# Mean-square minus squared mean over 16384 rows: the first load cut in two by partitions, the first store issued from GpSimd's queue

## The chip, the cores and the metric

The kernel runs on one core of a Trainium2 chip. The metric is the device time of one execution in microseconds (us). Three runs of the kernel before are shown, and one further execution was recorded by the hardware profiler.

## What is computed

The input holds 32 x 512 rows of 1024 float32 numbers, 64 MiB in all. For each row the kernel returns the mean of the squares minus the square of the mean, which is the row's variance.

```python
batch, seq, dim = 32, 512, 1024
x = np.random.randn(batch, seq, dim).astype(np.float32)

def reference(x):
    mean_sq = np.mean(x**2, axis=-1)
    sq_mean = np.mean(x, axis=-1)**2
    return (mean_sq - sq_mean).astype(np.float32)
```

## The kernel before

The 16384 rows are laid over 128 partitions, 128 rows to a partition. What the code calls a column is one row in each of the 128 partitions: 128 x 1024 float32, 512 KiB. There are 128 columns, in two blocks (`BLOCKS`): the first 16 columns take rows 0 to 2047, so that partition p holds rows 16p to 16p+15, and the other 112 columns take the remaining rows in the same way. Each block is stored by one DMA at the end of the program text.

**Loads.** All loads go through SyncE's queue, in program order (`load`, L45). The body has 13 groups of eight columns (`NGROUPS`, `GROUP`): one DMA of 4 MiB each, 32 KiB to a partition, into a pool `xpool` of three buffers. So the first three loads are issued at once, and the load of group g+3 waits until the computation on group g has freed its buffer. The last 24 columns are loaded into a tile of their own (`xt_end`) by six DMAs of 6, 6, 4, 3, 2 and 1 columns (`END_LOADS`), and four half columns of 256 KiB. In this text b0 to b5 are those six, and h0 to h3 the four halves.

The framework gives each DMA of SyncE's and ScalarE's queues one of eight completion semaphores in rotation. Where a semaphore is used again, the issue of the later DMA waits for the landing of the earlier one.

**Computation.** A column is done by one of two engines. ScalarE (`act_cols`, L121 and L129) makes two passes over it: a Copy that accumulates the negative mean, and a Square with that as bias that accumulates the variance. VectorE (`dve_half`, L111) makes two `bn_stats` of 512 elements for it. In the body ScalarE takes three columns of an even group and two of an odd one, VectorE the other five or six. Every instruction works on all 128 partitions.

**Joining.** The partial statistics of VectorE are joined to a variance by ten small GpSimd instructions (`join`, L90 to L102), which is called three times: for the odd groups, for the even groups, and for the first two loads of the end. The last VectorE columns are finished by `bn_aggr` on VectorE (L169, L179).

**Stores.** `store` (L52) writes 128 x 16 results of block 0 from ScalarE's queue and 128 x 112 results of block 1 from SyncE's queue. The framework places an instruction by its engine's program order and by priorities: in the built program the store of block 0 stands on ScalarE between its work on group 12 and its work on b0, where it waits for the second join on GpSimd.

```python
    store(nc.scalar, BLOCKS[0])
    store(nc.sync, BLOCKS[1])
```

Of the kernel before, what the change touches and what calls it, by code (L numbers as in the profile page):

```python
# [11 lines left out]
def kernel(  # L12
# [8 lines left out]
    nc = tc.nc  # L21
    P = nc.NUM_PARTITIONS
# [4 lines left out]
    xf = x.flatten_outer_dims()  # L27
    N, D = xf.shape
# [6 lines left out]
    BLOCKS = [(0, SMALL, 0), (SMALL, ncols - SMALL, SMALL * P)]  # L35

    def block_of(c):
        return next(b for b in BLOCKS if b[0] <= c < b[0] + b[1])

    def load(dst, c0, n, f0=0, f=D):  # L40

        b0, pitch, row0 = block_of(c0)
        assert c0 + n <= b0 + pitch
        ap = [[pitch * D, P], [D, n], [1, f]] if n > 1 else [[pitch * D, P], [1, f]]
        nc.sync.dma_start(  # L45
            out=dst,
            in_=dataclasses.replace(xf, offset=(row0 + c0 - b0) * D + f0, ap=ap),
        )

    def store(engine, block):  # L50
        b0, pitch, row0 = block
        engine.dma_start(  # L52
            out=dataclasses.replace(out, offset=row0, ap=[[pitch, P], [1, pitch]]),
            in_=mv[:, 1, b0 : b0 + pitch],
        )

    GROUP = 8
    NGROUPS = 13
    END0 = GROUP * NGROUPS
    ACT_OF_GROUP = (3, 2)  # L60

    END_LOADS = [6, 6, 4, 3, 2, 1]
    END_WHO = "AADDDDAADDDDDADDDADADA"
# [12 lines left out]
    def stats_block(name, groups, each):  # L76

        st = opool.tile([P, groups * each, 2, 6], FP32, name=name)
        return st

    def join(st, groups, each, first, step, skip):

        n = groups * each
        part = st.rearrange("p n h (e s) -> p n (h e) s", s=3)
        mean, m2 = part[:, :, :, 1], part[:, :, :, 2]
        two = opool.tile([P, n, 2], FP32, name=f"two{first}")
        mu = opool.tile([P, n, 1], FP32, name=f"mu{first}")
        dev = opool.tile([P, n, 4], FP32, name=f"dev{first}")
        g = nc.gpsimd
        g.tensor_tensor(out=two, in0=mean[:, :, 0:2], in1=mean[:, :, 2:4], op=ALU.add)  # L90
        g.tensor_tensor(out=mu, in0=two[:, :, 0:1], in1=two[:, :, 1:2], op=ALU.add)
        g.tensor_scalar(out=mu, in0=mu, scalar1=0.25, scalar2=None, op0=ALU.mult)  # L92
        g.tensor_tensor(out=dev, in0=mean, in1=mu.to_broadcast([P, n, 4]), op=ALU.subtract)  # L93
        g.tensor_tensor(out=dev, in0=dev, in1=dev, op=ALU.mult)  # L94
        g.tensor_scalar(out=dev, in0=dev, scalar1=D / 4.0, scalar2=None, op0=ALU.mult)  # L95
        g.tensor_tensor(out=dev, in0=dev, in1=m2, op=ALU.add)  # L96
        g.tensor_tensor(out=two, in0=dev[:, :, 0:2], in1=dev[:, :, 2:4], op=ALU.add)  # L97
        g.tensor_tensor(out=mu, in0=two[:, :, 0:1], in1=two[:, :, 1:2], op=ALU.add)
        var = mv[:, 1, first : first + groups * step].rearrange(
            "p (g k) -> p g k", k=step  # L100
        )[:, :, skip : skip + each]
        g.tensor_scalar(  # L102
            out=var,
            in0=mu.rearrange("p (g k) o -> p g (k o)", k=each),
            scalar1=1.0 / D,
            scalar2=None,
            op0=ALU.mult,
        )
# [4 lines left out]
    def dve_halves(stats, xcol):  # L113
        dve_half(stats, 0, xcol[:, :H])
        dve_half(stats, 1, xcol[:, H:])

    def act_cols(cols):

        s = D ** -0.5
        for i, (xcol, c) in enumerate(cols):  # L120
            nc.scalar.activation(  # L121
                out=junk[i],
                in_=xcol,
                func=ACTF.Copy,
                scale=-s / D,
                accum_out=neg_mean[:, c : c + 1],
            )
        for i, (xcol, c) in enumerate(cols):
            nc.scalar.activation(  # L129
                out=junk[3],  # L130
                in_=xcol,
                func=ACTF.Square,
                scale=s,
                bias=neg_mean[:, c : c + 1],
                accum_out=mv[:, 1, c : c + 1],
            )

    body = []
    for par in range(2):
        groups = len(range(par, NGROUPS, 2))  # L140
        each = GROUP - ACT_OF_GROUP[par]
        body.append((stats_block(f"stats{par}", groups, each), groups, each))
    for g in range(NGROUPS):
        c0 = g * GROUP
        xt = xpool.tile([P, GROUP, D], FP32, name="xt")
        load(xt, c0, GROUP)
        skip = ACT_OF_GROUP[g % 2]
        act_cols([(xt[:, k, :], c0 + k) for k in range(skip)])
        st, _, each = body[g % 2]
        for k in range(skip, GROUP):  # L150
            dve_halves(st[:, g // 2 * each + k - skip, :, :], xt[:, k, :])
    for par, (st, groups, each) in enumerate(body):
        join(st, groups, each, par * GROUP, 2 * GROUP, ACT_OF_GROUP[par])

# [4 lines left out]
    for b, n in enumerate(END_LOADS):  # L159
        load(xt_end[:, k : k + n, :] if n > 1 else xt_end[:, k, :], END0 + k, n)  # L160
        mine = range(k, k + n)
        act_cols([(xt_end[:, j, :], END0 + j) for j in mine if END_WHO[j] == "A"])
        for j in mine:
            if END_WHO[j] == "D" and b < nb:
                dve_halves(st_end[:, b * each + j - k - skip, :, :], xt_end[:, j, :])
            elif END_WHO[j] == "D":
                stats = spool.tile([P, 2, 6], FP32, name="stats")
                dve_halves(stats, xt_end[:, j, :])
                nc.vector.bn_aggr(out=mv[:, :, END0 + j], in_=stats)  # L169
        if b == nb - 1:  # L170
            join(st_end, nb, each, END0, step, skip)
        k += n
    for j in range(k, ncols - END0):
        stats = spool.tile([P, 2, 6], FP32, name="stats")
        for h in range(2):
            xh = xt_end[:, j, h * H : (h + 1) * H]
            load(xh, END0 + j, 1, h * H, H)
            dve_half(stats, h, xh)
        nc.vector.bn_aggr(out=mv[:, :, END0 + j], in_=stats)  # L179

    store(nc.scalar, BLOCKS[0])
    store(nc.sync, BLOCKS[1])


# [28 lines left out]
```

## Time and profile before

| what | value |
| --- | --- |
| runs, median (lowest to highest) | 165.49 us (165.44 to 165.92) |
| profiled execution, first to last instruction (span) | 163.5 us |
| median run minus profiled span | 2.0 us |
| VectorE (DVE) busy | 106.1 us, 65% |
| ScalarE (ACT) busy | 94.9 us, 58% |
| GpSimd (POOL) busy | 10.2 us, 6% |
| read from HBM | 67.11 MB, 411 GB/s over the span |
| share of SyncE's load queue of 16 DMA engines' time | 96.3% |

The profiled execution has no time of its own apart from its span; what lies around the span is taken as the 2.0 us by which the median run exceeds it. TensorE is not used. In the profile's lines DVE is VectorE, ACT ScalarE, POOL GpSimd and SP SyncE; SPq and ACTq are the instructions with which SyncE and ScalarE issue DMAs. `x10` behind a line means ten instructions, and what stands behind `<-` in brackets is what ended the engine's idle time.

### The profile page before, as it was taken

The numbers are of one execution on the slowest core, as the hardware profiler recorded it, in microseconds if no ns is written. First come the engines' busy times: TensorE is split into PE (matmuls) and PEld (weight loads), VectorE is DVE, ScalarE is ACT, GpSimd is POOL, SyncE is SP. The second block draws the span as 40 slices with busy tenths as digits, with TensorE's granted clock in tenths as the row PEclk, the third lists the DMA queues.
The fourth block names the chain that finished last, engine by engine and source line by source line (L and its number), as shares of the span: only waits on it lengthen the run. The fifth ranks groups of instructions, "written<-read, shape, count | busy, mean of one in ns | idle before, by whom it ended". The sixth has DMA issues, their size and how long they took to land.

```text
span 163.5 us, 462 instructions
## 1 busy us (share of the span) xinstructions
DVE 106.1 (65%) x182; ACT 94.9 (58%) x165; POOL 10.2 (6%) x34
## 2 busy tenths in 40 slices
DVE  0008559393793917949097682949559396859993
ACT  3008756195733937349390693809755195499892
POOL 0000000000000000000000000000000635302200
DMA  7899898998999999999999999999999999999970
GB/s 257 385 481 417 385 513 385 417 481 385 481 417 385 485 409 393 497 393 425 465 393 473 417 393 505 393 401 489 393 465 425 421 391 475 391 440 409 408 291 14
DMA packets 3602, 67.19 MB, mean 411 GB/s; under 512 B 656, under 2 KB 656, under 8 KB 1296
## 3 DMA queue, kind: packets, MB, share of 16 engines
q1 hardware_dynamic: 3456, 67.17, 96.3%
q10 hardware_dynamic: 144, 0.01, 0.1%
q14 instruction: 2, 0.02, 0.0%
HBM read 67.11 MB, written 0.07 MB: 411 GB/s over the span
## 4 chain that ended last, share of the span: by engine, by line
DMA 79%; DVE 11%; ACT 8%; issue 0%; SPq 0%
DMA xt<-in_x_dram 62%; DMA xt_end<-in_x_dram 17%; DVE stats L111 10%; ACT junk L129 4%; ACT junk L121 4%; DVE mv L179 0%; SPq L45 0%
## 5 line engine op out<-in xcount | busy, mean ns | idle before, releaser
L111 DVE BATCH_NORM_STATS2 stats<-xt 128x6 f32<-128x512 f32 x142 | 85.5, 678 | 50.7 <-DMA xt<-in_x_dram 50.7
L121 ACT ACTIVATE junk<-xt 128x1024 bf16<-128x1024 f32 x33 | 34.5, 1046 | 59.2 <-DMA xt<-in_x_dram 59.2
L129 ACT ACTIVATE junk<-xt,neg_mean 128x1024 bf16<-128x1024 f32 x33 | 37.7, 1142 | 0.6
L111 DVE BATCH_NORM_STATS2 stats_end<-xt_end 128x6 f32<-128x512 f32 x16 | 9.7, 680 | 3.7 <-DMA xt_end<-in_x_dram 3.7
L121 ACT ACTIVATE junk<-xt_end 128x1024 bf16<-128x1024 f32 x8 | 8.4, 1046 | 5.0 <-POOL mv L102 4.2
L111 DVE BATCH_NORM_STATS2 stats<-xt_end 128x6 f32<-128x512 f32 x16 | 10.1, 666 | 0.1
L129 ACT ACTIVATE junk<-xt_end,neg_mean 128x1024 bf16<-128x1024 f32 x8 | 9.2, 1144 | 0.2
L90 POOL TENSOR_TENSOR two<-stats 128x72 f32<-128x72 f32 (+1 forms) x2 | 0.8, 406 | 131.3 <-DVE stats L111 131.3
L129 ACT ACTIVATION_READ_ACCUMULATOR junk<-xt,neg_mean 128x1 f32 x33 | 6.2, 186 | 0.0
L121 ACT ACTIVATION_READ_ACCUMULATOR junk<-xt 128x1 f32 x33 | 6.2, 186 | 0.0
L121 ACT ACT_TABLE_LOAD x1 | 1.3, 1283 | 0.7 <-PEq L197 0.7
L121 ACT ACTIVATION_READ_ACCUMULATOR junk<-xt_end 128x1 f32 x8 | 1.5, 186 | 0.0
L129 ACT ACTIVATION_READ_ACCUMULATOR junk<-xt_end,neg_mean 128x1 f32 x8 | 1.5, 186 | 0.0
L95 POOL TENSOR_SCALAR dev<-dev 128x144 f32<-128x144 f32 (+2 forms) x3 | 1.4, 472 | 0.3
L169 DVE BATCH_NORM_AGGREGATE mv<-stats 128x2 f32<-128x12 f32 x6 | 1.2, 203 | 0.1
L94 POOL TENSOR_TENSOR dev<-dev 128x144 f32<-128x144 f32 (+2 forms) x3 | 1.1, 362 | 0.2
L96 POOL TENSOR_TENSOR dev<-dev,stats 128x144 f32<-128x144 f32 (+1 forms) x2 | 1.1, 528 | 0.2
L93 POOL TENSOR_TENSOR dev<-stats,mu 128x144 f32<-128x144 f32 (+1 forms) x2 | 0.9, 470 | 0.2
L102 POOL TENSOR_SCALAR mv<-mu 128x36 f32<-128x36 f32 (+2 forms) x3 | 0.9, 287 | 0.3
L92 POOL TENSOR_SCALAR mu<-mu 128x36 f32<-128x36 f32 (+2 forms) x3 | 0.9, 284 | 0.3
L97 POOL TENSOR_TENSOR two<-dev 128x72 f32<-128x72 f32 (+2 forms) x3 | 0.8, 276 | 0.2
L90 POOL TENSOR_TENSOR two<-stats_end 128x16 f32<-128x16 f32 x1 | 0.2, 233 | 8.9 <-DVE stats_end L111 8.9
(9 smaller groups left out, 2.7 us busy)
## 6 DMA issues: line engine op xcount, KB each, us to landing
xt<-in_x_dram SPq DMA_DIRECT2D x13, 4096.0 KB, 22.2
xt_end<-in_x_dram SPq DMA_DIRECT2D x2, 3072.0 KB, 32.2
xt_end<-in_x_dram SPq DMA_DIRECT2D x1, 2048.0 KB, 40.0
xt_end<-in_x_dram SPq DMA_DIRECT2D x1, 1536.0 KB, 43.2
xt_end<-in_x_dram SPq DMA_DIRECT2D x1, 1024.0 KB, 45.1
xt_end<-in_x_dram SPq DMA_DIRECT2D x4, 256.0 KB, 15.3
xt_end<-in_x_dram SPq DMA_DIRECT2D x1, 512.0 KB, 36.7
out_dram<-mv SPq DMA_DIRECT2D x1, 56.0 KB, 1.6
```

The lines of the kernel that those rows point to most:

```text
L90: g.tensor_tensor(out=two, in0=mean[:, :, 0:2], in1=mean[:, :, 2:4], op=ALU.add)
L92: g.tensor_scalar(out=mu, in0=mu, scalar1=0.25, scalar2=None, op0=ALU.mult)
L93: g.tensor_tensor(out=dev, in0=mean, in1=mu.to_broadcast([P, n, 4]), op=ALU.subtract)
L94: g.tensor_tensor(out=dev, in0=dev, in1=dev, op=ALU.mult)
L95: g.tensor_scalar(out=dev, in0=dev, scalar1=D / 4.0, scalar2=None, op0=ALU.mult)
L96: g.tensor_tensor(out=dev, in0=dev, in1=m2, op=ALU.add)
L97: g.tensor_tensor(out=two, in0=dev[:, :, 0:2], in1=dev[:, :, 2:4], op=ALU.add)
L102: g.tensor_scalar(out=var, in0=mu.rearrange("p (g k) o -> p g (k o)", k=each), scalar1=1.0 / D, scalar2=None, op0=ALU.mult,)
L111: nc.vector.bn_stats(out=stats[:, h, :], in_=xh)
L121: nc.scalar.activation(out=junk[i], in_=xcol, func=ACTF.Copy, scale=-s / D, accum_out=neg_mean[:, c : c + 1],)
L129: nc.scalar.activation(out=junk[3], in_=xcol, func=ACTF.Square, scale=s, bias=neg_mean[:, c : c + 1], accum_out=mv[:, 1, c : c + 1],)
L169: nc.vector.bn_aggr(out=mv[:, :, END0 + j], in_=stats)
```

## The change

`load` gets a first partition and a number of partitions. The load of group 0 becomes two DMAs on SyncE's queue: partitions 0 to 15 (512 KiB), then partitions 16 to 127 (3.5 MiB), both with 32 KiB to a partition. All other loads stay as they are. The store of block 0 is issued from GpSimd's queue instead of ScalarE's.

```diff
-    def load(dst, c0, n, f0=0, f=D):
+    def load(dst, c0, n, f0=0, f=D, p0=0, p=P):
...
-        ap = [[pitch * D, P], [D, n], [1, f]] if n > 1 else [[pitch * D, P], [1, f]]
+        ap = [[pitch * D, p], [D, n], [1, f]] if n > 1 else [[pitch * D, p], [1, f]]
         nc.sync.dma_start(
             out=dst,
-            in_=dataclasses.replace(xf, offset=(row0 + c0 - b0) * D + f0, ap=ap),
+            in_=dataclasses.replace(
+                xf, offset=(row0 + p0 * pitch + c0 - b0) * D + f0, ap=ap
+            ),
         )
...
+    FIRST = (16, 112)
...
-        load(xt, c0, GROUP)
+        p0 = 0
+        for p in FIRST if g == 0 else (P,):
+            load(xt[p0 : p0 + p], c0, GROUP, p0=p0, p=p)
+            p0 += p
...
-    store(nc.scalar, BLOCKS[0])
+    store(nc.gpsimd, BLOCKS[0])
     store(nc.sync, BLOCKS[1])
```

In the built program the changes of order are these. SyncE issues the two pieces one after the other, ahead of groups 1 and 2. VectorE's first instruction waits for both pieces; ScalarE's table load now waits for the second piece and its first activation for the first piece. The load of group 3 waits for both pieces as well as for the work on group 0. On GpSimd the store stands between the second and the third join. ScalarE has one instruction less. SyncE's and ScalarE's queues together issue as many DMAs as before (one load more, one store less), so the loads of the end shift by one semaphore up to b5, and the halves and the last store keep theirs; h2, which waited for the first store's landing, now waits for b0's.

## Prediction

> **What bounds the kernel now.** I read the page's slices and queues first, then the chain of waits, then the timeline at both ends and a table of stretches.
>
> ```profile
> DVE 106.1 (65%) x182; ACT 94.9 (58%) x165; POOL 10.2 (6%) x34
> ...
> DMA  7899898998999999999999999999999999999970
> GB/s 257 385 481 417 385 513 385 417 481 385 481 417 385 485 409 393 497 393 425 465 393 473 417 393 505 393 401 489 393 465 425 421 391 475 391 440 409 408 291 14
> ...
> q1 hardware_dynamic: 3456, 67.17, 96.3%
> ...
> DMA 79%; DVE 11%; ACT 8%; issue 0%; SPq 0%
> ```
>
> No compute engine is busy for more than 65% of the span, but the load queue is for 96.3%. The DMA engines fall short of nine tenths only in scattered slices and at the two ends. The chain is loads for 79%; its VectorE and ScalarE pieces in the body lie beside loads that keep running.
>
> ```profile
> 30.00:130.00 100.00, 66.25 (x110) 57.01 (x100) 1.85 (x5) 1.00 1.00 432
> ```
>
> In the body (the last two columns are DMA share and GB/s) the stream has no gap: 432 GB/s at a share of 1.00. Whatever time the stream loses anywhere cannot be caught up.
>
> ```profile
> 0.72 29.34 SPq L45 DMA_DIRECT2D xt<-in_x_dram  x5
> 12.74 6.03 DVE L111 BATCH_NORM_STATS2 stats<-xt 128x6 f32<-128x512 f32 x10 [12.74 <-DMA xt<-in_x_dram]
> ...
> 22.45 7.22 DVE L111 BATCH_NORM_STATS2 stats<-xt 128x6 f32<-128x512 f32 x12 [3.68 <-DMA xt<-in_x_dram]
> 22.45 1.06 ACT L121 ACTIVATE junk<-xt 128x1024 bf16<-128x1024 f32 x1 [2.81 <-DMA xt<-in_x_dram]
> ```
>
> These timeline rows give start, length and, in brackets, the idle time before. Group 0 lands at 12.74 and group 1 at 22.45: 9.71 us for a 4 MiB load in steady flow. The first load takes 12.00 us from its issue (chain), 2.29 more.
>
> ```profile
> 140.86 0.37 ACTq L52 DMA_DIRECT2D out_dram<-mv  x1
> 141.28 1.06 ACT L121 ACTIVATE junk<-xt_end 128x1024 bf16<-128x1024 f32 x1 [4.20 <-POOL mv L102]
> ...
> 149.71 0.23 POOL L90 TENSOR_TENSOR two<-stats_end 128x16 f32<-128x16 f32 x1 [8.88 <-DVE stats_end L111]
> ...
> 153.38 1.06 ACT L121 ACTIVATE junk<-xt_end 128x1024 bf16<-128x1024 f32 x1 [0.71 <-DMA xt_end<-in_x_dram]
> ...
> 157.83 1.37 DVE L111 BATCH_NORM_STATS2 stats<-xt_end 128x6 f32<-128x512 f32 x2
> ...
> 160.98 0.35 SPq L52 DMA_DIRECT2D out_dram<-mv  x1
> ```
>
> The first store holds ScalarE for 4.20 us at the beginning of the end stage, but ScalarE waits for a load again at 153.38: it has caught up. VectorE gets the last loads, ends at 160.84, and the last store follows.
>
> The profiled span is 163.5 us and the median run 165.49, so I add differences to 165.49 and leave the 2.0 us around the span alone. What a measurement of this kernel can tell from no change is about 0.3%, 0.5 us.
>
> **The first load in two pieces.** The bytes are the same. One DMA issue is added on SyncE, 0.33 us (median of this line), before the issues of groups 1 and 2. It lies beside piece one's transfer; without that cover it would cost 0.33. Computation cannot start earlier: VectorE's first instruction needs all 128 partitions and waits for both pieces. So the split can act only through the rate and the start of the stream.
>
> The trace has no load to fewer than 128 partitions. Two readings fit every load it has: time follows total bytes (4 MiB in 9.71 us), or time follows bytes per partition (32 KiB in 9.71 us). They part here. Piece one is an eighth of the bytes but still 32 KiB to each of its partitions: 9.71 / 8 = 1.21 us by the first reading, 9.71 by the second. The packet records speak between the two: a group's load is 128 packets of 32 KiB, sixteen at a time, each 1.21 us long, so one partition can take its 32 KiB in 1.21 us. Sixteen neighbours at once are slower if neighbours share a way into SBUF. If they share in eights (128 partitions over 16 streams), piece one takes eight rounds of 1.21, 9.71; if in fours, four, 4.85; if not at all, one. No row is nearer to one end, so I take the middle of 1.21 and 9.71, 5.46 us: **4.25 us lost**. Both ends, 0 and 8.50, stay for the range.
>
> [...]
>
> Piece two is seven sixteenth-rows per stream, 7 x 1.21 = 8.50 us when its streams stay apart. With seven partitions to a stream in place of eight, the streams need not be spread as in a full load. If every packet shared its way with one other throughout, it would take 17.0. So the loss lies between 0 and 8.5; 112 partitions are nearer to the full load, which loses nothing, than to the small piece, so I take a third: **2.8 us lost**. Groups 1 to 12 and the end loads are as before and follow in the same queue, so the 4.25 + 2.8 = 7.05 us pass on to every later landing.
>
> Could compute or a late issue add to that? The load of group 3 is issued when group 0 is done, at 19.67; the queue is dry at 32.18, when group 2 lands. The first load's excess of 2.29 off leaves 10.2 us of cover. All of this shifts together. ScalarE's table load, 1.28 us at 0.72 now in idle time, will run after the second piece has landed: cover falls to 8.9 us, and ScalarE has 2.81 idle before group 1. Cost 0; without cover, 1.28.
>
> **The first store on GpSimd.** ScalarE loses a wait of 4.20 us and an issue of 0.37. What is late there next is load b1, for which VectorE waits until 144.78; from b3 (153.38) ScalarE starts where it starts now. Gain 0 at the end. On GpSimd the store waits for the second join, done at 140.83, which stands right before it, and for ScalarE's columns 8 to 15, long done. Behind it is only the third join, which cannot start before VectorE is ready at 149.71, and takes until 152.83; only the last store at 160.98 needs it. Cover: 8.88 idle plus 8.15 after it, 17.0 us. No row shows GpSimd issuing a DMA. Its nearest rows are ScalarE's issue of the same bytes (0.37) and that store's time from issue to landing (9.0), both under 17.0. I take a cost of 0; a gain is excluded, since nothing that ends late waits for this store. [...] Slower or not, the sum is the same while the 17 us hold.
>
> SyncE's load issues wait for reused semaphores: 12.1 us of h2's wait are for this store's landing.
>
> ```profile
> SPq L45 <- DMA out_dram<-mv: 12.1, 1, 12.1
> ```
>
> Now h2 waits for b0, and h2 and h3 are issued as soon as b1 has landed, by 144.78 instead of 150.3. They move about 157, behind b2 to b5, so they are no earlier: gain 0. The 8 KiB themselves pass the same DMA engines either way (0.1% of their span): 0.
>
> **Sum:** 165.49 + 4.25 + 2.8 + 0 = 172.5 us.
>
> **Rivals.**
> - *An earlier start, no sharing* (not slower). Sixteen partitions accept the full 432 GB/s, and the small first DMA flows sooner than a large one. Of the first load's 2.29 us beyond steady flow, the last store, a small transfer, still shows 1.6 from issue to landing; so at most 0.7 can go: 164.8. For it: the stream is so full that every tenth counts, and the first slice moves only 257 GB/s. Against: SyncE's issue takes 0.33 to 0.43 us whatever the load's size. It decides if piece one lands within about 1.21 us of flow.
> - *Nothing happens.* Sixteen partitions accept the full rate and the start does not depend on size: 165.5. For it: sixteen packets fly at a time in a full load too, and each has one partition. Against: which sixteen is chosen by the hardware, and nothing says that neighbours go together.
> - *Piece two as bad as piece one*: each of its seven rounds takes 5.46 us: 38.2 + 5.46 - 9.71 = 34 us lost, 199.4. It would need every round of all streams to fall on neighbours.
> - *GpSimd is held longer than 17.0 us*: then the end slips by what is beyond. Against: nine microseconds is the longest row for this store. Its small chance is in the last case.
>
> **How the numbers follow.** Loss through sharing 0.80, earlier start 0.09, nothing 0.08, the last two 0.03. Faster 0.09, same 0.08, slower 0.83. The forecast is the likeliest case, 172.5. The range begins where packets of piece one share their ways in pairs and piece two loses nothing (+1.21, 166.7) and ends where piece one takes a full load's time with piece two as taken (8.5 + 2.8, 176.8). What is left out is the two cases that are not slower, 0.17, and about 0.03 above.
>
> **What the profile after should show.** Group 0's first instructions on VectorE start at about 19.8 instead of 12.74 and group 1's 9 to 10 us later; the early slices show far less than 400 GB/s, then 432 as before; the step from one group to the next stays 9.7. ScalarE's table load stands at about 18 or later. ScalarE has no wait for POOL L102, VectorE's wait of 8.88 on the third join stays, and the last stage has the same lengths 7 us later. I am wrong in the main step if group 0 starts by 13.2, wrong in its size if it starts outside 14 to 24, and wrong on the store if the end stage, from b0's landing to the last store, differs in length by over 0.5 us.

## The result and the profile after

The changed kernel takes 174.81 us (median of four runs, 174.52 to 174.93) against 165.47 for the kernel before: 9.3 us more, a ratio of 1.0559 with a 95% interval of 1.0545 to 1.0573. The profiled execution, the fastest of the four, has a span of 172.4 us, 8.9 more than before.

The page of the kernel after, in the parts shown of before:

```profile
DVE 106.1 (62%) x182; ACT 95.1 (55%) x165; POOL 10.8 (6%) x35
...
DMA  8989899999998999999999999999999999999980
GB/s 122 236 243 251 243 441 403 464 388 471 388 471 380 466 418 435 456 403 464 388 471 395 456 403 456 441 411 464 395 464 403 433 439 394 445 409 439 402 326 13
...
q1 hardware_dynamic: 3472, 67.17, 96.5%
q14 instruction: 2, 0.02, 0.0%
q0 software_dynamic: 32, 0.01, 0.0%
```

Read the DMA and GB/s rows together. The first five slices (4.3 us each) move 122 to 251 GB/s, while the DMA engines count as busy as ever. A packet that crawls counts as busy (in the packet records the 16 of piece one take 3.4 to 4.0 us each for 32 KiB, where 1.21 was usual before); its rate shows only in bytes. Queue 1's share even rises, 96.3 to 96.5%, over a longer span. The 32 packets of queue 0 are the store that GpSimd now issues.

From the DMA issues of the kernel after (KB each, us from issue to landing), the two pieces of the first load:

```profile
xt<-in_x_dram SPq DMA_DIRECT2D x1, 3584.0 KB, 21.3
...
xt<-in_x_dram SPq DMA_DIRECT2D x1, 512.0 KB, 6.9
```

From its timeline (start, length, what; in brackets the idle time before), the start and the end:

```profile
0.73 39.02 SPq L45 DMA_DIRECT2D xt<-in_x_dram  x6
22.49 1.28 ACT L124 ACT_TABLE_LOAD   x1 [22.49 <-DMA xt<-in_x_dram]
22.52 6.03 DVE L114 BATCH_NORM_STATS2 stats<-xt 128x6 f32<-128x512 f32 x10 [22.52 <-DMA xt<-in_x_dram]
...
32.13 7.22 DVE L114 BATCH_NORM_STATS2 stats<-xt 128x6 f32<-128x512 f32 x12 [3.58 <-DMA xt<-in_x_dram]
...
149.89 0.73 POOL L54 DMA_DIRECT2D out_dram<-mv  x1 [0.30 <-POOL mv L105]
...
153.56 1.06 ACT L124 ACTIVATE junk<-xt_end 128x1024 bf16<-128x1024 f32 x1 [2.71 <-DMA xt_end<-in_x_dram]
...
158.50 0.23 POOL L93 TENSOR_TENSOR two<-stats_end 128x16 f32<-128x16 f32 x1 [7.88 <-DVE stats_end L114]
...
166.62 1.37 DVE L114 BATCH_NORM_STATS2 stats<-xt_end 128x6 f32<-128x512 f32 x2
...
169.76 0.35 SPq L54 DMA_DIRECT2D out_dram<-mv  x1
```

Piece one lands at 0.73 + 6.9 = 7.6 us. Group 0 can start at 22.52, 9.78 later than before, and group 1 follows 9.61 behind it. The last store is issued at 169.76, 8.78 later. So all of the loss arises before 22.5 us, and about one microsecond of it is got back on the way.

### The profile page after: what moved, and what is told of

Its sections match the earlier page's. It is cut to its first block, busy times and chain, and to the rows that moved or that the text cites. A ratio compares the mean times of both kernels' runs of the same rounds, so it can differ in the third digit from the quotient of the medians.

```text
span 172.4 us, 468 instructions
## 1 busy us (share of the span) xinstructions
DVE 106.1 (62%) x182; ACT 95.1 (55%) x165; POOL 10.8 (6%) x35
## 3 DMA queue, kind: packets, MB, share of 16 engines
q1 hardware_dynamic: 3472, 67.17, 96.5%
## 4 chain that ended last, share of the span: by engine, by line
DMA 83%; ACT 8%; DVE 6%; SPq 1%; issue 0%
DMA xt<-in_x_dram 61%; DMA xt_end<-in_x_dram 22%; DVE stats L114 6%; ACT junk L132 4%; ACT junk L124 4%; SPq L45 1%; DVE mv L185 0%
## 5 line engine op out<-in xcount | busy, mean ns | idle before, releaser
L124 ACT ACT_TABLE_LOAD x1 | 1.3, 1283 | 22.5 <-DMA xt<-in_x_dram 22.5
L54 POOL DMA_DIRECT2D out_dram<-mv x1 | 0.7, 733 | 0.3 <-POOL mv L105 0.3
```

The lines of the kernel that those rows point to most:

```text
L124: nc.scalar.activation(out=junk[i], in_=xcol, func=ACTF.Copy, scale=-s / D, accum_out=neg_mean[:, c : c + 1],)
```

## The experiments

In this part the packet records are the trace's own list of DMA packets, each with its start, length and size; a stream is one of the sixteen sequences of packets that run side by side; where the expectations count rows for a stream, a row is the 32 KiB of one partition.

Two theories were held against each other. W supposes that the partitions of SBUF hang on a limited number of ways, that neighbours share one, and that a load is as fast as the number of ways its partitions reach; no trace shows the ways themselves. B: a load's time follows the bytes per partition, 32 KiB in 9.7 us. Further rivals: the pieces are small or uneven (U), the rows that are read set the rate (S), GpSimd's store costs part (G).

**Each edit alone.** The split alone:

```diff
-    store(nc.gpsimd, BLOCKS[0])
+    store(nc.scalar, BLOCKS[0])
```

> The first load in pieces of 16 and 112 partitions, the first store back on ScalarE's queue. Theory W (destination partitions share a limited number of ways into SBUF, so neighbours slow each other): the whole of the loss is here, 174 to 175 us, and group 0 lands near 22.5 as with both edits. Rival G (part of the loss is GpSimd's: its DMA or the end of the kernel): 0.4 us or more below the kernel with both edits, 174.4 or less.

Measured: 174.65 us, ratio 1.055 (1.0536 to 1.0565). VectorE starts on group 0 at 22.70 us. That is within 0.2 us of the kernel with both edits, so the loss is the split's.

The store alone is the kernel before with `store(nc.gpsimd, BLOCKS[0])`:

> One first load of 128 partitions, the first store on GpSimd's queue. W and the prediction: 165.5 us, within 0.3% of before; ScalarE's wait of 4.20 us for POOL is gone and its last instruction ends where it did. Rival G: 165.9 us or more.

Measured: 165.43 us, ratio 0.9994 (0.9985 to 1.0003): no difference. Its timeline shows the edit doing all that it says:

```profile
141.12 0.73 POOL L52 DMA_DIRECT2D out_dram<-mv  x1 [0.30 <-POOL mv L102]
...
144.80 1.06 ACT L121 ACTIVATE junk<-xt_end 128x1024 bf16<-128x1024 f32 x1 [2.72 <-DMA xt_end<-in_x_dram]
...
149.73 0.23 POOL L90 TENSOR_TENSOR two<-stats_end 128x16 f32<-128x16 f32 x1 [7.88 <-DVE stats_end L111]
...
153.38 1.06 ACT L121 ACTIVATE junk<-xt_end 128x1024 bf16<-128x1024 f32 x1 [1.27 <-DMA xt_end<-in_x_dram]
```

The wait for POOL is gone from ScalarE; it waits for loads instead, and at 153.38 it is where it was before, to the hundredth. GpSimd is held 0.73 us and its third join starts at 149.73 instead of 149.71.

**The same sizes on other partitions.** Two kernels load group 0 in two pieces of 64 partitions with the store on ScalarE. One takes neighbours:

```diff
-    FIRST = (16, 112)
+    FIRST = (64, 64)
```

> Pieces of 64 and 64 neighbouring partitions, store on ScalarE. W: partitions 0 to 63 reach half of the ways, and so do 64 to 127, so each piece takes about 9.7 us instead of 4.85, group 0 lands at about 22.4 and the time is 173.5 to 175.5. Rival B (time follows bytes per partition, 32 KiB in 9.7 us, whatever the partitions): the same, 19.4 for both pieces, 174 to 176. Rival U (the loss comes from small or uneven pieces: one row for a stream, seven rows for a stream): four rows a stream in both, so little loss, 165.5 to 167.

The other takes the even partitions and then the odd ones:

```diff
+            for p0 in (0, 1):
+                load(xt[p0:P:2], c0, GROUP, p0=p0, p=P // 2, ps=2)
```

> Also 64 and 64 partitions, but the even ones first and then the odd ones; store on ScalarE. Both pieces span all 128 partitions. W: each piece reaches all ways, 4.85 us each, no loss: 165.5 to 166 and group 0 lands at 12.7 to 13.2. Rival B: 32 KiB to a partition in both pieces, 19.4 us together, 174 to 176 as with neighbouring halves. Rival U: 165.5 to 167 in both.

Measured: neighbours 176.12 us, ratio 1.0644 (1.0629 to 1.0658); even and odd 165.91, ratio 1.0029 (1.002 to 1.0039). VectorE's first instruction on group 0, first with neighbours, then with even and odd partitions:

```profile
23.76 6.03 DVE L114 BATCH_NORM_STATS2 stats<-xt 128x6 f32<-128x512 f32 x10 [23.76 <-DMA xt<-in_x_dram]
```

```profile
13.23 6.03 DVE L114 BATCH_NORM_STATS2 stats<-xt 128x6 f32<-128x512 f32 x10 [13.23 <-DMA xt<-in_x_dram]
```

Two pieces, four rows to a stream and 32 KiB to a partition in both kernels, and 10.5 us between them. This rules out B and U. The neighbours are slower than W expected, 176.12 against 173.5 to 175.5: in the packet records most of their packets take 2.56 us, a little over 2 x 1.21 = 2.42, the estimate for two packets on one way under W. The 0.4 us by which even and odd miss the kernel before is at the start (13.23 against 12.74): the longest issue of a body load on SyncE is 0.58 us there (as with neighbouring halves) against 0.43, and the first packet starts at 2.07 us against 1.72 in the packet records. Its later packets take 1.21 us each, so it is no sharing.

**The disputed cost by itself.** Twelve more loads stand behind the last load of the kernel before, each issued when the one before it has landed, into columns that nobody reads any more. Nothing is left out of the computation; the kernel is only longer.

```diff
+    to = xt_end[:, 16:24, :]
+    nc.sync.dma_start(out=to, in_=rows(128))
+    nc.sync.dma_start(out=to[0:16:4], in_=rows(4))
+    nc.sync.dma_start(out=to[0:4], in_=rows(4))
...
```

> The kernel before, with twelve more loads behind its last one, each issued when the one before it has landed, all into the last columns of xt_end that nobody reads any more; 32 KiB to a partition in all. Within one size all read the same rows of x, and only the destination partitions differ. Latency beyond flow is about 2.3 us. [...] Rival B: 9.7 + latency for every one. Rival S (the source rows or their pitch set the rate): equal times within one size, whatever the destination.

The step from one issue to the next is the time of a load from issue to landing (SyncE's timeline):

```profile
160.81 0.33 SPq L188 DMA_DIRECT2D xt_end<-in_x_dram  x1
...
172.80 0.74 SPq L189 DMA_DIRECT2D xt_end<-in_x_dram  x1
176.55 0.30 SPq L190 DMA_DIRECT2D xt_end<-in_x_dram  x1
182.65 0.63 SPq L191 DMA_DIRECT2D xt_end<-in_x_dram  x1
186.31 0.26 SPq L192 DMA_DIRECT2D xt_end<-in_x_dram  x1
192.36 0.54 SPq L193 DMA_DIRECT2D xt_end<-in_x_dram  x1
196.96 0.51 SPq L194 DMA_DIRECT2D xt_end<-in_x_dram  x1
201.55 0.33 SPq L195 DMA_DIRECT2D xt_end<-in_x_dram  x1
208.44 0.54 SPq L196 DMA_DIRECT2D xt_end<-in_x_dram  x1
213.29 0.50 SPq L197 DMA_DIRECT2D xt_end<-in_x_dram  x1
225.81 0.50 SPq L198 DMA_DIRECT2D xt_end<-in_x_dram  x1
233.28 0.32 SPq L199 DMA_DIRECT2D xt_end<-in_x_dram  x1
```

The last load ends in SyncE's final wait for it:

```profile
SPq L225 <- DMA xt_end<-in_x_dram: 17.1, 1, 17.1
```

| destination partitions | KiB | issue to landing, us | less 2.29 of latency, us |
| --- | --- | --- | --- |
| all 128 | 4096 | 11.99 | 9.70 |
| 0, 4, 8, 12 (twice) | 128 | 3.75, 3.66 | 1.46, 1.37 |
| 0, 1, 2, 3 (twice) | 128 | 6.10, 6.05 | 3.81, 3.76 |
| 0, 16, 32, 48 | 128 | 4.60 | 2.31 |
| 0, 32, 64, 96 | 128 | 4.59 | 2.30 |
| 0 to 15 | 512 | 6.89 | 4.60 |
| 0, 4, ... 60 | 512 | 4.85 | 2.56 |
| 0 to 63 | 2048 | 12.52 | 10.23 |
| 0, 2, ... 126 | 2048 | 7.47 | 5.18 |
| 16 to 127 | 3584 | about 17.4 (0.32 + 17.1) | 15.1 |

The 2.29 is what the first load of the kernel before took beyond 9.71; that it holds for the smaller loads is an estimate. Within one size the same rows of x are read, so S is out: the same 128 KiB take 3.7, 4.6 or 6.1 us by destination alone. B, which has 9.7 for every row of the last column, is out too. Neighbours are the dearest of each size, as W has it: four partitions four apart take 1.4 us, near one packet of 1.21; four that are 16 or 32 apart 2.3 and 16 that are four apart 2.56, near two (2.42); four neighbours 3.8; 16 neighbours 4.60, near four (4.84). Nor are neighbours queued one behind another in one stream: in the packet records the four packets of each of the four-partition loads start within 0.7 us of each other and run side by side, 1.8 to 1.9 us each at 0, 4, 8, 12 and 2.8 to 3.7 at 0, 1, 2, 3. 64 neighbours take longer for 2 MiB than all 128 partitions for 4. Two rows do not fit such counting: four neighbours alone cost 2.4 us over four separate ones, not the 3.63 of three more packets of 1.21, so this short burst went faster than four packets end to end; and 112 neighbours take longer than all 128.

In bytes per second, with 2.29 taken off, partitions 0 to 15 took 114 GB/s (512 KiB in 6.89 - 2.29) and 0 to 63 205 (2 MiB in 12.52 - 2.29). A transfer need not write all 128 partitions to go faster: the even ones, spread from 0 to 126, take 2 MiB in 7.47 - 2.29 us, 405 GB/s. The 112 partitions from 16 on come to 243 GB/s (3.5 MiB in 15.1). If they reach seven eighths of the ways, W alone has 9.7 us for them (3.5 MiB at seven eighths of 432 GB/s), as for all 128; so by this estimate the count of ways does not account for their 15.1. It may be that which packets fly together matters as well, but no record here says which partition a packet goes to.

**More pieces, other pieces.** Eight pieces of 16, `FIRST = (16,) * 8`:

> The first load as eight pieces of 16 neighbouring partitions, store on ScalarE. W: every piece as slow as piece one, some 4.8 us each, 38.7 in all, 29 us more than one load: 194 to 196 us in the worst case, less if streams that get ahead spread over other ways (185 to 195). Rival U, in the form that only the uneven count of the pair 16 and 112 costs: about 166. Rival B: 8 x 9.7 = 78 us for group 0, about 233.

Measured: 191.85 us, ratio 1.1587 (1.1562 to 1.1612). VectorE's start on group 0:

```profile
40.04 6.03 DVE L114 BATCH_NORM_STATS2 stats<-xt 128x6 f32<-128x512 f32 x10 [40.04 <-DMA xt<-in_x_dram]
```

With the first issue at 0.72 and 2.29 of latency off, that is 37.0 us, 4.6 for each piece. It is piece one's cost eight times over, not that of a cold or uneven start.

The 112 first, `FIRST = (112, 16)`:

> Pieces of 112 and then 16 neighbouring partitions; store on ScalarE. W: both pieces are still crowded; streams done early with the big piece start on the small one, so somewhat less than with 16 first, 171 to 174 us. U in the form that a start with a small piece costs: no loss, 165.5 to 166.5.

Measured: 174.96 us, ratio 1.0566 (1.0541 to 1.0591), a little above the expected 171 to 174. U's form is out. That 16 first is the dearer order shows where group 0 lands: VectorE starts on it at 21.97 us here, at 22.70 in the split alone. By the end the gain is lost, since one later interval between groups is long in this kernel:

```profile
50.80 7.22 DVE L114 BATCH_NORM_STATS2 stats<-xt 128x6 f32<-128x512 f32 x12 [3.70 <-DMA xt<-in_x_dram]
61.48 1.88 DVE L114 BATCH_NORM_STATS2 stats<-xt 128x6 f32<-128x512 f32 x3 [3.47 <-DMA xt<-in_x_dram]
```

That is 10.68 us, against 9.70 in the split alone; the paragraph on the sum comes back to it.

A cut by columns, each half to all 128 partitions:

```diff
-        load(xt, c0, GROUP)
+        half = GROUP // 2
+        for k in (0, half) if g == 0 else ():
+            load(xt[:, k : k + half, :], c0 + k, half)
+        if g:
+            load(xt, c0, GROUP)
```

> The first load cut by columns, 4 and 4, each to all 128 partitions; store on ScalarE. W and B: no loss, 165.5 us, since all ways are used and 16 KiB to a partition takes half of 9.7; VectorE and ScalarE start on the first half at about 7.9 us, which gains nothing, since the load stream sets the end. U (two pieces cost something in themselves): 166 or more.

Measured: 165.57 us, ratio 1.0002 (0.9992 to 1.0012). In its timeline VectorE starts on group 0 at 7.83 us, yet group 1 comes when it did:

```profile
7.83 1.29 DVE L111 BATCH_NORM_STATS2 stats<-xt 128x6 f32<-128x512 f32 x2 [7.83 <-DMA xt<-in_x_dram]
12.72 4.84 DVE L111 BATCH_NORM_STATS2 stats<-xt 128x6 f32<-128x512 f32 x8 [3.60 <-DMA xt<-in_x_dram]
22.43 1.88 DVE L111 BATCH_NORM_STATS2 stats<-xt 128x6 f32<-128x512 f32 x3 [4.87 <-DMA xt<-in_x_dram]
```

A second DMA as such costs nothing here, and starting computation five microseconds sooner gains nothing either, since the stream sets the end. No version tried was faster than the kernel before.

## Why the prediction was right, and which term was too small

**What bounds the kernel** held in the main. What the stream lost at the start arrived at the end, less about a microsecond, which is looked at below; that lost time "cannot be caught up" was too strong by that much.

**Piece one** was taken at 5.46 us, a loss of 4.25. It landed 6.9 us after its issue; less 2.29 of latency that is 4.6, a loss of 3.4. The prediction's own case of ways shared in fours, 4.85, was nearer than the middle of the two readings.

**Piece two** was the mis-sized term: 2.8 us, a third of the way to 8.5, with the reason that 112 partitions are near to 128. Piece two landed at 22.5, 14.9 after piece one, against 8.5 without sharing: 6.4 us lost. The load of 112 partitions by itself says the same, 17.4 - 2.29 - 8.5 = 6.6. In the packet records of the kernel after, its packets take 1.5 to 3.3 us instead of 1.21. Nearness in count is not nearness in time. That packets in flight shared ways here, as the prediction's upper bound for this piece supposed, fits their lengths; which of them met on which way no record shows.

**The sum.** 3.4 + 6.4 = 9.8, which is group 0's delay of 9.78; 7.05 was predicted, with group 0 at 19.8 instead of 22.52. Of this, 8.9 reaches the span. So the 172.5 owes part of its nearness to luck: piece two was 3.6 too small, but piece one was 0.85 too large, and about a microsecond that the prediction passed on to every later landing did not arrive. Its step of 9.7 from one group to the next overlooked that in the kernel before one interval between groups is long; in the kernel after it is not (VectorE's timeline around 51 to 62 us, first before, then after):

```profile
51.69 6.03 DVE L111 BATCH_NORM_STATS2 stats<-xt 128x6 f32<-128x512 f32 x10 [2.58 <-DMA xt<-in_x_dram]
62.19 1.28 DVE L111 BATCH_NORM_STATS2 stats<-xt 128x6 f32<-128x512 f32 x2 [4.47 <-DMA xt<-in_x_dram]
```

```profile
51.55 7.22 DVE L114 BATCH_NORM_STATS2 stats<-xt 128x6 f32<-128x512 f32 x12 [3.68 <-DMA xt<-in_x_dram]
61.26 1.28 DVE L114 BATCH_NORM_STATS2 stats<-xt 128x6 f32<-128x512 f32 x2 [2.49 <-DMA xt<-in_x_dram]
```

10.50 us against 9.71. In the packet records two 8 KiB packets of the instruction queue fall at 55.8 and 57.1 us in the kernel before, and at 56.1 and 65.7 after. In both kernels one load packet near them takes 1.88 us. Before, the last sixteen packets of a load end within 0.4 to 0.6 us of each other until then and within about 1.1 from then on. After, they are 1.0 or more apart from the start, and stay so. So the delay may have hit a stream that was already ahead of the slowest one, and been hidden. The other kernels agree only in part. With the store alone, the columns cut, and even and odd partitions the interval is long too (10.56, 10.49, 10.64), and with 64 and 64 neighbours and with eight pieces, whose streams are 0.6 apart, it is 10.0. But with the 112 first the streams are 1.1 apart and it is 10.68 all the same. No experiment was made for this; the cause of the microsecond stays open.

**Covers.** Group 3's load was issued in time: groups 1 to 2 and 2 to 3 are 9.71 apart. ScalarE's table load moved to 22.49 and cut ScalarE's wait before group 1 to 1.44, near the 2.81 - 1.28 = 1.53 that follows from the prediction's numbers.

**The store** cost 0 as predicted. GpSimd was held 0.73 us of 17.0, and the issue of h2 moved earlier without effect. The wait of 8.88 on the third join, which the forecast called VectorE's and unchanged, is GpSimd's wait for VectorE; it fell to 7.88, since GpSimd issues the store in that time. From b0's landing to the last store's issue it is 23.50 us after (146.26 to 169.76) and 23.51 before (137.47 to 160.98).

**The rivals.** The earlier start did not come: the first packet of piece one starts at 1.73 us in the packet records, 1.72 before, although the load is an eighth as large. "Nothing happens" fell with the first five slices. "Piece two as bad as piece one" was taken as remote and would be 34 us; eight pieces of 16, each of sixteen neighbours, show a loss of 26.4 us.

## What to carry to other kernels

Cut a load along its free dimension, not into blocks of neighbouring partitions: the column cut cost nothing (ratio 1.0002), the cuts into blocks 9 to 26 us, because the load stream sets the end. When a share of busy DMA engines stays at nine tenths and the bytes per second fall, as here to 122 to 251 GB/s, look at which partitions the loads in flight write. A wait that an engine makes up before the end, as ScalarE's 4.20 us here, is worth nothing.

## What the runs showed of the hardware that was not expected

A load to the 64 even partitions reached 405 GB/s, nearly the 432 of the body before, where 64 neighbours reached 205. SyncE took longer to issue some shapes of the twelve added loads: 0.51 to 0.74 us for loads to 4 or 16 partitions with a step, 0.26 to 0.33 for 4, 16, 112 or 128 neighbours, and 0.50 for 64 partitions of either kind. A DMA issued by GpSimd held that engine 0.73 us, and it moved its 8 KiB in 16 packets of 512 bytes, where ScalarE's queue took 128 packets of 64 bytes (each queue had 16 packets of 4 bytes besides).
